# Decoder trunk on one Trainium2 core: weight halves split four half slabs ahead in five buffers, the RG-LRU product on VectorE, its gate weights on ScalarE's queue

## The chip, the cores and the metric

The kernel runs on one core of one Trainium2 chip. The core has a matrix engine (TensorE; PE in the profile, PEld for its weight loads), a vector engine (VectorE; DVE), an engine for activation functions (ScalarE; ACT), a general one (GpSimd; POOL) and one that only issues transfers (SyncE; SP). Each works through its own queue of instructions in order, and they wait for each other by semaphores. On chip there are two memories, SBUF for operands and PSUM for what TensorE adds up; 16 DMA engines move data between SBUF and the chip's main memory, HBM. The metric is device time in microseconds (us) for one run of the whole program.

## The reference

Two layers of a decoder trunk on 256 tokens of width 1024, all in float32. Every layer has three sub-layers, each modulated by vectors that come from a conditioning vector `c`, and each followed by a residual sum and a layer norm:

```python
mod = silu(c) @ mod_w[l] + mod_b[l]                  # nine vectors of 1024
x = LN(ALPHA * x + 0.5 * (1 + g1) * swiglu(x * (1 + sc1) + sh1))
x = LN(ALPHA * x +       (1 + g2) * mixer (x * (1 + sc2) + sh2))
x = LN(ALPHA * x + 0.5 * (1 + g3) * swiglu(x * (1 + sc3) + sh3))
```

`swiglu` is `(silu(gate) * up) @ w_out` with 2816 hidden columns. The mixer of layer 0 ("even") runs an RG-LRU and a gated linear attention (GLA) side by side; that of layer 1 ("odd") is latent attention. The RG-LRU is what one part of the change touches:

```python
r, i = sigmoid(x @ w_a + b_a), sigmoid(x @ w_x + b_x)     # blocks of 64 x 64
log_a = -8 * r * softplus(-lam)
u = sqrt(-expm1(2 * log_a)) * (i * x)
h[t] = exp(log_a[t]) * h[t-1] + u[t]                      # over the 256 tokens
```

## The kernel before

Activations lie transposed: 128 features on the partitions, 256 tokens along a row, eight such tiles (`k` or `f`) for the width of 1024.

**Weights.** All weight matrices are cut into tiles of 128x128 and stored in the order in which TensorE uses them (`PLAN`, lines 108 to 162). Sixteen tiles are a slab of 1 MB, eight a half slab. Float32 precision comes from splitting each operand into a high and a low half of a reduced type (float32r): a product is three matmuls, high x high, high x low and low x high (`mm3`, lines 403 to 409; each 128x128 by 256 columns). So each half slab of weights, once it has landed, is split: ScalarE copies it into `whi` (line 338), VectorE subtracts that copy and writes the rest into `wlo` (line 339). One half slab serves 24 matmuls.

**Class Stream** (lines 300 to 398) runs this pipeline. Raw slabs land in `wraw`, five buffers, which they share with the modulation weights (`modw`, 1 MB each, two columns' worth). `next` hands out weights; when a new half slab `s` is reached it calls `conv_to(s + 1 + AHEAD)`, with `AHEAD = 3`, which emits the splits up to three half slabs further on, after `dma_to` has emitted the transfers of the slabs for them and of up to `RAW = 4` beyond. `whi` and `wlo` have four buffers each, so a split can start when TensorE has finished the half slab four before it. Right behind the splits, `reduce` (line 388) multiplies a modulation weight slab by `silu(c)` and sums it on VectorE; these sums are due by a table (`MOD_TARGETS`) and their results go to the modulation vectors.

**Order of work.** The program only lists instructions. A planner then puts them in order for each engine: it goes through them by priority, which is the place in the listing, simulates when each could start, and gives each engine the ready instruction of highest priority. `tc.high_priority()` moves an instruction forward in that order, `manual_schedule` fixes the order of some engines, and `queue_behind` puts one instruction behind another. On the chip each engine then keeps that order, whatever is ready.

**Buffers in SBUF.** `flat0` and `flat1` (line 452) are two areas of 8 x `FROW` floats a row, `FROW = 320`, used in turn for partial sums, for the scaled `y` of a boundary (`self.ya`, line 546, eight rows of 256 tokens and two extra columns), and in the mixers. The conditioning vector first lands in a buffer of the tag `junk` (line 275), whose other use is the discarded output of `reduce`.

**Boundary** (lines 514 to 678) is what happens between sub-layers. While the last projection's eight tiles `f` come out of TensorE, `tile_out` computes `y = psum * gate + ax` on VectorE (line 581), squares it on ScalarE (585), and adds up sums and squares (588, 589). To keep the statistics exact, the values of tile 0 are used as a shift: `shift_out` (line 559) copies `y` of tile 0 on ScalarE (`yr`, 564), TensorE averages it over the features (566), ScalarE copies the result (`shift`, 569), GpSimd subtracts it from the seven other residual tiles `ax` (571), and VectorE from tile 0 itself (572). Each `y` of tiles 1 to 7 needs its `ax` after that subtraction.

**Even mixer** (lines 790 to 1055). Its steps run in the order of `EVEN_STEPS`; `R` and `S` are the two halves of the RG-LRU, four tiles each. `rglru` loads a tile's gate weights (`rgt`, line 829, 128 KB, from SyncE's queue, two buffers), convolves, multiplies by them (835, 836), applies the gates on ScalarE, and then for all four tiles at once, 128x1024, computes the decay and the input on VectorE (844 to 850). The last product, by the convolved `x`, is on GpSimd (851); the scans over the tokens follow on VectorE (853).

## Time and profile before

| | before |
|---|---|
| median of three runs | 1037.29 us (1035.79 to 1043.17) |
| the profiled execution: its own time | 1033.83 us |
| its span, first to last instruction | 1032.1 us |
| PE busy | 995.5 us, 96% |
| PEld busy | 972.8 us, 94% |
| DVE busy | 884.7 us, 86% |
| ACT busy | 612.5 us, 59% |
| POOL busy | 54.8 us, 5% |
| read from HBM | 256.18 MB |

A row of a timeline reads: start in us from the span's start, busy us, engine, source line, operation, what it writes and reads, how many in a row, and in brackets the idle time before it and what ended that. A row of waits reads: engine and line, what it waited for, total us, how often, the longest. A row of a stretch reads: its limits and length, busy us and number of instructions for PE, PEld, DVE, ACT and POOL, the granted clock as a share, the busy share of the DMA engines, and GB/s. A row for one line of the source gives the shortest, median and longest duration in ns and the first and last start.

### The profile page before, as it was taken

How to read it: one execution, taken by the hardware profiler on the slowest of the kernel's cores; microseconds unless marked ns; L12 is line 12 of the kernel's file. 1: busy time of each engine (PE TensorE's matmuls, PEld its weight loads, DVE VectorE, ACT ScalarE, POOL GpSimd, SP SyncE). 2: the span in 40 equal slices, each digit the busy share in tenths (PEclk: the TensorE clock that was granted, in tenths of full speed). 3: DMA queues.
4: the chain of work that ended last, by engine and by line, in shares of the span. 5: the costliest groups of instructions: out<-in, count | busy, mean ns of one | idle time of the engine just before them, and what ended most of it. 6: DMA issues, size and time to landing. Idle time of an engine off the chain costs nothing.

```text
span 1032.1 us, 20703 instructions
## 1 busy us (share of the span) xinstructions
PE 995.5 (96%) x8338; PEld 972.8 (94%) x8338; DVE 884.7 (86%) x1491; ACT 612.5 (59%) x1023; POOL 54.8 (5%) x72
## 2 busy tenths in 40 slices
PE   6999999999999989999999999999999999999995
PEld 5999999998899979999999999999998889999995
DVE  5789999797998989999998899998888799666664
ACT  4746654567886656745545665455559666545543
POOL 0000010000001020000030000002000200000200
PEclk9999999999999999999999999999999999999998
DMA  9998798554466943699977469898743146665621
GB/s 342 366 339 319 257 368 309 208 204 169 170 264 242 350 185 142 245 361 373 365 279 286 166 251 371 322 359 321 286 167 129 73 164 245 246 224 187 243 83 41
DMA packets 38578, 258.57 MB, mean 251 GB/s; under 512 B 4289, under 2 KB 6849, under 8 KB 7762
## 3 DMA queue, kind: packets, MB, share of 16 engines
q1 hardware_dynamic: 38482, 257.25, 66.7%
q8 instruction: 65, 1.06, 0.4%
q14 instruction: 31, 0.25, 0.1%
HBM read 256.18 MB, written 1.05 MB: 249 GB/s over the span
## 4 chain that ended last, share of the span: by engine, by line
PE 82%; DVE 11%; issue 2%; ACT 2%; DMA 2%; POOL 0%; SPq 0%; DVEq 0%; ACTq 0%
PE mm L409 25%; PE mm L407 25%; PE mm L408 25%; DVE wlo L339 4%; DVE junk L388 2%; DMA wraw<-modw 1%; ACT whi L338 1%; DVE flat L557 1%; DVE yy L581 1%; PE ax L408 1%; PE ax L407 1%; PE ax L409 1%; DVE acc L589 1%; DVE flat L731 0%; DMA rgt<-rgw 0%
## 5 line engine op out<-in xcount | busy, mean ns | idle before, releaser
L339 DVE TENSOR_TENSOR wlo<-wraw,whi 128x1024 fp32r<-128x1024 f32 x340 | 416.7, 1233 | 81.3 <-ACT whi L338 80.8
L338 ACT ACTIVATE whi<-wraw 128x1024 fp32r<-128x1024 f32 x340 | 357.6, 1058 | 212.4 <-PE mm L408 138.0
L407 PE MATMUL mm<-uhi,whi 128*128 128x256 f32 x1672 | 461.4, 278 | 11.5 <-ACT uhi L444 6.0
L409 PE MATMUL mm<-uhi,wlo 128*128 128x256 f32 x1672 | 460.1, 277 | 3.6 <-DVE wlo L339 3.6
L408 PE MATMUL mm<-ulo,whi 128*128 128x256 f32 x1672 | 462.1, 277 | 0.7 <-DVE ulo L445 0.6
L407 PEld LDWEIGHTS mm<-uhi,whi 128*128 128x128 f32 x1672 | 313.6, 188 | 14.9 <-ACT uhi L444 7.9
L409 PEld LDWEIGHTS mm<-uhi,wlo 128*128 128x128 f32 x1672 | 313.8, 188 | 4.2 <-DVE wlo L339 4.1
L408 PEld LDWEIGHTS mm<-ulo,whi 128*128 128x128 f32 x1672 | 314.8, 188 | 1.5 <-DVE ulo L445 1.2
L409 PE MATMUL mm<-hhi,wlo 128*128 128x256 f32 x704 | 194.6, 276 | 1.9 <-DVE wlo L339 1.9
L408 PE MATMUL mm<-hlo,whi 128*128 128x256 f32 x704 | 194.4, 276 | 0.0
L407 PE MATMUL mm<-hhi,whi 128*128 128x256 f32 x704 | 194.3, 276 | 0.0
L388 DVE CUSTOM_DVE_ANT_0 junk<-wraw,cact,cols 128x1024 bf16<-128x1024 f32 x144 | 184.9, 1284 | 5.7 <-DMA wraw<-modw 5.0
L409 PEld LDWEIGHTS mm<-hhi,wlo 128*128 128x128 f32 x704 | 132.1, 188 | 2.3 <-DVE wlo L339 2.3
L407 PEld LDWEIGHTS mm<-hhi,whi 128*128 128x128 f32 x704 | 132.2, 188 | 0.0
L408 PEld LDWEIGHTS mm<-hlo,whi 128*128 128x128 f32 x704 | 132.2, 188 | 0.0
L571 POOL TENSOR_TENSOR ax<-ax,shift 128x256 f32<-128x256 f32 x42 | 42.2, 1039 | 734.7 <-ACT shift L569 734.7
L444 ACT ACTIVATE hhi<-h 128x256 fp32r<-128x256 f32 x88 | 35.9, 413 | 44.3 <-DVE h L702 43.2
L585 ACT ACTIVATE ysq<-yy 128x256 f32<-128x256 f32 x42 | 17.4, 414 | 51.8 <-DVE yy L581 50.0
L702 DVE SCALAR_TENSOR_TENSOR h<-mm,sg 128x256 f32<-128x256 f32 x75 | 30.9, 418 | 7.9 <-PE mm L409 7.9
L581 DVE SCALAR_TENSOR_TENSOR yy<-mm,gate,ax 128x256 f32<-128x256 f32 x48 | 22.8, 478 | 16.2 <-PE mm L409 15.0
L445 DVE TENSOR_TENSOR hlo<-h,hhi 128x256 fp32r<-128x256 f32 x88 | 36.0, 417 | 0.0
L429 ACT ACTIVATE sg<-mm 128x256 f32<-128x256 f32 x75 | 27.4, 366 | 3.0 <-DVE h L702 1.7
(288 smaller groups left out, 1088.1 us busy)
## 6 DMA issues: line engine op xcount, KB each, us to landing
wraw<-wst SPq DMA_DIRECT2D x169, 1024.0 KB, 5.8
wraw<-modw SPq DMA_DIRECT2D x71, 1024.0 KB, 6.5
wraw<-modw SPq DMA_DIRECT2D x2, 512.0 KB, 5.4
yy<-xT SPq DMA_DIRECT2D x8, 128.0 KB, 6.8
wraw<-wst SPq DMA_DIRECT2D x2, 512.0 KB, 7.9
rgt<-rgw SPq DMA_DIRECT2D x8, 128.0 KB, 3.7
outT<-yy SPq DMA_DIRECT2D x3, 256.0 KB, 2.6
outT<-yy SPq DMA_DIRECT2D x2, 128.0 KB, 2.6
```

The lines of the kernel that those rows point to most:

```text
L338: act.activation(hi, raw, AF.Copy)
L339: i = vec.tensor_tensor(lo, raw, hi.bitcast(F32), SUB)
L388: i = vec.tensor_tensor_reduce(junk, t, cact, 1.0, col("mod_b", (l * NMOD + v) * KD + j), MULT, ADD, self.modcols[(l, v)][:, j:j + 1])
L407: pe.matmul(ps, hi, mh, start=start, stop=False, skip_group_check=shared)
L408: pe.matmul(ps, hi, ml, start=False, stop=False, skip_group_check=shared)
L409: pe.matmul(ps, lo, mh, start=False, stop=stop, skip_group_check=shared)
L429: i = act.activation(out, in_, func, **kw)
L444: act.activation(hi, src, AF.Copy)
L445: vec.tensor_tensor(lo, src, hi.bitcast(F32), SUB)
L571: pool.tensor_tensor(ax[:, j, :], ax[:, j, :], shift, SUB)
L581: vec.scalar_tensor_tensor(y, ps, self.gate[:, f:f + 1], ax[:, f, :], MULT, ADD)
L702: vec.scalar_tensor_tensor(h, pu, bu, sg, ADD, MULT)
```

## The change

- `AHEAD` goes from 3 to 4, and `whi` and `wlo` from four buffers to five: splits are listed one half slab earlier and have a buffer more. The raw buffers stay at five.
- `FROW` goes from 320 to 272. The rows of `self.ya` then start 258 floats apart instead of 320.
- The conditioning vector's first buffer moves from `junk` to `flat0`.
- The copy `yr` in `shift_out` gets high priority.
- In `rglru`, `rgt` has three buffers instead of two, its transfers are issued by ScalarE instead of SyncE, and the product of line 851 runs on VectorE instead of GpSimd.

```diff
-FROW = 320
+FROW = 272
...
-    whi = ctx.enter_context(tc.tile_pool(name="whi", bufs=4))
+    whi = ctx.enter_context(tc.tile_pool(name="whi", bufs=5))
...
-    wlo = ctx.enter_context(tc.tile_pool(name="wlo", bufs=4))
+    wlo = ctx.enter_context(tc.tile_pool(name="wlo", bufs=5))
...
-    crow = T(wk, [1, DM], tag="junk", bufs=1)
+    crow = T(main, [1, DM], tag="flat0")
...
-        AHEAD = 3
+        AHEAD = 4
...
-                self.ya = [flat(q, F32R).rearrange("p (k c) -> p k c", k=KD) for q in range(2)]
+                self.ya = [flat(q, F32R)[:, :KD * (SEQ + 2)].rearrange("p (k c) -> p k c", k=KD) for q in range(2)]
...
-            act.activation(yr, y, AF.Copy)
+            with tc.high_priority():
+                act.activation(yr, y, AF.Copy)
...
-                    mm3(ps[:, :SEQ + 2], W.next((m, k, f)), [t[:, k, :SEQ + 2] for t in self.ya], k == 0, k == KD - 1)
+                    mm3(ps[:, :SEQ + 2], W.next((m, k, f)), [t[:, k, :] for t in self.ya], k == 0, k == KD - 1)
...
-                    rgt = T(ew, [P, 2, P], tag="rgt")
-                    sync.dma_start(rgt, rgw[j])
+                    rgt = T(ew, [P, 2, P], tag="rgt", bufs=3)
+                    act.dma_start(rgt, rgw[j])
...
-                pool.tensor_tensor(tz, tz, xc, MULT)
+                vec.tensor_tensor(tz, tz, xc, MULT)
```

## The prediction

> **What bounds the kernel now.** I read the page's busy shares first, then who TensorE waited for, then those waits one by one in the timeline, and last the queues that ended them.

> ```profile
> PE 995.5 (96%) x8338; PEld 972.8 (94%) x8338; DVE 884.7 (86%) x1491; ACT 612.5 (59%) x1023; POOL 54.8 (5%) x72
> PE mm L409 <- DVE wlo L339: 6.5, 6, 1.5
> PE mm L407 <- ACT uhi L444: 6.0, 1, 6.0
> PE mm L407 <- DVE yy L581: 3.1, 2, 1.9
> PE mm L407 <- ACT whi L338: 2.2, 2, 1.4
> ```

> The first row gives 1032.1 - 995.5 = 36.6 us in which TensorE does nothing, and the change takes no matmul away, so this is all there is to win. The other rows (total us, times, longest) say what it waited for: 6.5 us for low halves of weights (`wlo`, VectorE), 3.1 for the boundary's `yy`; the 6.0 and the 2.2 lie in the start, before the first two and at two later weight slabs. The single waits in the timeline, with the idle time in brackets:

> ```profile
> 125.20 0.38 PE L409 MATMUL mm<-uhi,wlo 128*128 128x256 f32 x1 [1.04 <-DVE wlo L339]
> 164.93 0.38 PE L409 MATMUL mm<-hhi,wlo 128*128 128x256 f32 x1 [1.21 <-DVE wlo L339]
> 171.35 0.39 PE L409 MATMUL mm<-hhi,wlo 128*128 128x256 f32 x1 [0.68 <-DVE wlo L339]
> 273.93 0.38 PE L409 MATMUL mm<-uhi,wlo 128*128 128x256 f32 x1 [1.02 <-DVE wlo L339]
> 278.45 0.38 PE L409 MATMUL mm<-uhi,wlo 128*128 128x256 f32 x1 [1.50 <-DVE wlo L339]
> 349.79 0.39 PE L409 MATMUL mm<-ya,wlo 128*128 128x256 f32 x1 [1.06 <-DVE wlo L339]
> 378.10 0.38 PE L407 MATMUL mm<-uhi,whi 128*128 128x256 f32 x1 [1.20 <-DVE yy L581]
> 386.07 0.38 PE L407 MATMUL mm<-uhi,whi 128*128 128x256 f32 x1 [1.92 <-DVE yy L581]
> 835.65 0.46 PE L597 MATMUL ax<-acc,ones_dm 128*128 128x256 f32 x1 [1.33 <-DVE acc L588]
> 837.03 0.70 PE L598 MATMUL ax<-acc,ones_dm 128*128 128x256 f32 x2 [0.71 <-DVE acc L589]
> ```

> Six waits for `wlo` (1.04 + 1.21 + 0.68 + 1.02 + 1.50 + 1.06 = 6.51 us), two for `yy` (3.12), two in the statistics behind the odd mixer (2.04). Busy time by stretch (us, PE, PEld, DVE, ACT, POOL, then clock and DMA) shows which stage each lies in:

> ```profile
> 60.00:70.00 10.00, 10.00 (x90) 10.00 (x90) 6.69 (x12) 5.29 (x8) 0.00 (x0) 1.00 0.97 357
> 160.00:170.00 10.00, 8.79 (x77) 8.60 (x77) 10.00 (x28) 5.90 (x10) 0.00 (x0) 1.00 0.73 265
> 240.00:250.00 10.00, 10.00 (x45) 8.17 (x44) 8.54 (x14) 7.60 (x11) 0.00 (x0) 1.00 0.40 130
> 270.00:280.00 10.00, 7.48 (x63) 7.09 (x62) 10.00 (x14) 6.64 (x12) 2.40 (x1) 1.00 0.30 105
> 340.00:350.00 10.00, 8.94 (x79) 8.74 (x78) 10.00 (x18) 7.57 (x13) 0.00 (x0) 1.00 0.95 351
> 1020.00:1030.00 10.00, 0.84 (x4) 0.30 (x2) 7.06 (x18) 4.94 (x11) 2.09 (x3) 0.68 0.31 104
> ```

> Where TensorE waits for weights, VectorE is busy 10.00 of 10 us; ahead of those stretches it has room (6.69 of 10 at 60, 8.54 at 240). The last row is the tail, 9.16 us of idle TensorE in which no weight is converted: the change leaves it.

> **Five buffers, four ahead.** What holds a conversion back where VectorE has room:

> ```profile
> ACT whi L338 <- PE mm L408: 138.0, 124, 2.6
> 47.45 1.06 ACT L338 ACTIVATE whi<-wraw 128x1024 fp32r<-128x1024 f32 x1 [0.72 <-PE mm L408]
> 50.17 1.06 ACT L338 ACTIVATE whi<-wraw 128x1024 fp32r<-128x1024 f32 x1 [1.66 <-PE ax L408]
> 48.55 1.23 DVE L339 TENSOR_TENSOR wlo<-wraw,whi 128x1024 fp32r<-128x1024 f32 x1 [1.16 <-ACT whi L338]
> ```

> In 124 cases ScalarE sat until a matmul gave a buffer back, so the fifth buffer will be used. Two conversions in that state lie 50.17 - 47.45 = 2.72 us apart, TensorE's time for a half slab. With four buffers a half slab starts when the one four before it is done and is due three later, 3 x 2.72 = 8.16 us; it is ready at 48.55 + 1.23 = 49.78, 2.33 us after its start, so the lead is 5.83 us. Five buffers make it 8.55.

> What that closes depends on VectorE. The work is the same; one conversion (1.23 us) is done while there is room and is then missing from the busy stretch, and in VectorE's queue each `wlo` stands one half slab earlier, ahead of work whose results TensorE wants later. Counted wait by wait:
> - 125.20: the lead was full at 60 us, where VectorE has 3.3 us of room in ten. 1.04 is less than the 1.23 taken out of the queue: closed, 1.04.
> - 164.93 and 171.35, 1.89 together: the stretch at 160 shows VectorE full, and the first wait has used up the lead, so I count the one conversion alone, 1.23, and leave 0.66. Bounds: 0 (VectorE is the limit and the wait only moves) and 1.89.

> The raw buffers stay five. A half slab converted earlier gives its raw buffer back earlier, which can only bring the next transfer forward; at the start TensorE waits for transfers and modulation sums, the same in both, so I count 0 there.

> **The product from GpSimd to VectorE.** It occurs twice, once for each half of the RG-LRU:

> ```profile
> 269.09 1.22 DVE L850 SCALAR_TENSOR_TENSOR ya<-ya,ya 128x1024 f32<-128x1024 f32 x1
> 270.39 2.40 POOL L851 TENSOR_TENSOR ya<-ya 128x1024 f32<-128x1024 f32 x1 [61.11 <-DVE ya L850]
> 270.56 3.31 DVE L339 TENSOR_TENSOR wlo<-wraw,whi 128x1024 fp32r<-128x1024 f32 x1
> 311.47 3.33 POOL L851 TENSOR_TENSOR ya<-ya 128x1024 f32<-128x1024 f32 x1 [38.68 <-DVE ya L850]
> 314.83 2.44 DVE L853 TENSOR_TENSOR_SCAN flat<-ya,ya 128x256 f32<-128x256 f32 x4 [2.30 <-POOL ya L851]
> ```

> VectorE's queue gets one 128x1024 product; the same shape takes 1.22 on line 850. In the first half the `wlo` beside the product took 3.31 instead of 1.23, so taking the product off GpSimd gives 2.08 back and costs 1.22: VectorE is 0.86 us earlier. This very `wlo` is the one of the wait at 273.93. With the conversion done ahead in the room at 240 (1.46 us) that is 0.86 + 1.23 = 2.09 against waits of 1.02 + 1.50 = 2.52; and the scans, which stood before the next `wlo`, are no longer held either. I take 2.52, with 0.86 as the low bound. [...]

> In the second half VectorE waited 2.30 for GpSimd before the scans and will compute 1.22: 1.08 us earlier, into the stretch that stays busy until 349.79. With the earlier conversion, 1.08 + 1.23 = 2.31, more than the wait of 1.06: closed. Bounds 0 and 1.06.

> **Gate weights on ScalarE's queue, three buffers.**

> ```profile
> SPq L829 <- PE ax L836: 4.3, 3, 3.0
> 257.70 0.38 SPq L325 DMA_DIRECT2D wraw<-wst  x1
> rgt<-rgw SPq DMA_DIRECT2D x8, 128.0 KB, 3.7
> 252.56 1.06 ACT L338 ACTIVATE whi<-wraw 128x1024 fp32r<-128x1024 f32 x1 [0.51 <-PE mm L986]
> ```

> SyncE was held 4.3 us in three waits for a buffer that the gate matmuls read, and a weight transfer stood behind the longest, at 257.70. That hold moves to ScalarE, in front of conversions and the gates' activations, though with three buffers the third load needs no wait. No row shows an issue on ScalarE; SyncE's is 0.38, so eight cost about 3.0, and with all the old waits 7.3 us of ScalarE's time. I count 0: ScalarE waited for TensorE itself at 252.56, it is busy 7.60 of 10 us at 240, and the lead covers one hold of 3.0. Without that cover the cost is 7.3; on the other side SyncE, freed by up to 3.0 us, gains nothing, because no wait above is for `wraw`.

> **The copy `yr` at high priority.**

> ```profile
> 372.55 0.48 DVE L581 SCALAR_TENSOR_TENSOR yy<-mm,gate,ax 128x256 f32<-128x256 f32 x1 [0.59 <-PE mm L409]
> 372.49 1.06 ACT L338 ACTIVATE whi<-wraw 128x1024 fp32r<-128x1024 f32 x1 [0.99 <-PE mm L408]
> 373.45 0.40 ACT L564 ACTIVATE shift<-yy 128x256 fp32r<-128x256 f32 x1
> 375.22 0.39 ACT L569 ACTIVATE shift<-ax 128x256 f32<-128x256 f32 x1 [0.41 <-PE ax L566]
> 375.68 6.67 POOL L571 TENSOR_TENSOR ax<-ax,shift 128x256 f32<-128x256 f32 x7 [60.88 <-ACT shift L569]
> L571 POOL TENSOR_TENSOR ax<-ax,shift x42: 717/919/1783, 151.2 to 977.6; 128x256 f32<-128x256 f32 x42
> ```

> `yy` of tile 0 is there at 373.03; the copy starts at 373.45 because a conversion was put ahead of it. So 0.42 goes from the way to the shift, the subtractions on GpSimd and the `yy` that TensorE waited 1.20 for. Bounds 0 and 3.12 (the wait of 1.92 stands behind the same seven subtractions; no row says how much of it is theirs). In the boundaries behind an FFN TensorE did not wait for `yy`: 0.

> Rows of `flat` packed closer (258 instead of 320 columns), the conditioning row in `flat0` instead of `junk`: same instructions, same shapes; 0.

> **Sum.** 1.04 + 1.23 + 2.52 + 1.06 + 0.42 = 6.27 us. The profiled execution has a span of 1032.1 and a time of 1033.83, 3.46 below the median 1037.29 of the runs (1035.79 to 1043.17). On its own time 1027.6; on the median 1031.0.

> **Rivals.**
> - VectorE stays the limit: the waits move along the busy stretches, and only its own saving counts, 0.86 + 1.06 = 1.92. Or the planner leaves the conversions where they were, and the edit does not do what it says. For: three of the six stretches above have VectorE at 10.00. Against: 124 conversions started on a freed buffer. Time 1035.4, between 1033.5 and 1037.5.
> - The boundaries close too: all six weight waits, both `yy` waits and the two behind the odd mixer, 6.51 + 3.12 + 2.04 = 11.67. For: one conversion less stands among that work. Against: a conversion per 2.72 us stays in VectorE's queue there. Time 1025.6, up to 1028.
> - Slower: collisions in the mixers' boundaries. The order of VectorE's queue is new, and one conversion stands nearer to the seven subtractions. Their duration ranges from 0.717 to 1.783 and was 6.67 / 7 = 0.95 in the even boundary. If every one meets a VectorE instruction that went first, each takes 1.783: 7 x 0.83 = 5.8 us per boundary, straight onto the `yy` that TensorE waits for, and 11.6 in the two behind the mixers. With the rest of the gain, 5.85, this gives 1043.0; without it 1048.9. It decides if VectorE has a two-input instruction running at each subtraction's start; against it, the median of all 42 is 0.919, so most meet none. [...]

> **How the numbers follow.** Forecast 0.55 (1028.5 to 1033.5), VectorE the limit 0.20, boundaries too 0.14, slower 0.11. The range 1026 to 1038 holds the first two, half of the third and little of the fourth, 0.82. One per cent, about what a measurement of this kernel can tell from no change, is 10.4 us: faster means under 1026.9. Two thirds of the third case lie there, 0.09, and the low edge of the forecast with the runs' spread adds 0.08: 0.17. Slower means over 1047.7, half of the fourth case: 0.06. Within: 0.77.

> **What would show it.** Right: the waits of `mm L409` for `wlo` fall from 6.5 to about 0.7; the lines of 125, 274, 278 and 350 are gone; no line 851 on GpSimd, no `wlo` of 3.31, the scans wait for nothing; TensorE idle near 30 us with its busy time unchanged. The copy step is right if the wait of 1.20 shrinks by about 0.4. Wrong: `wlo` waits of the same total at later places (first rival); conversions whose durations differ from 1.06 and 1.23, which would speak of the new addresses; ScalarE held by a gate load for longer than the lead of 8.55; subtractions near 1.78 (third rival).

## The result: 0.5% slower, and the profile after

The changed kernel takes 1042.63 us (median of 20 runs, 1035.89 to 1047.03); the kernel before, run beside it, 1036.74 (20 runs, 1034.21 to 1043.17). The ratio is 1.005, with a 95% interval of 1.0036 to 1.0064. The forecast was 1031.0, in a range that ended at 1038: the sign was wrong. The profiled execution of the changed kernel has a time of its own of 1047.03 us, the longest of the 20, and a span of 1045.3; that of before had 1033.83 and 1032.1. So the two profiles lie 13.2 us apart, where the medians lie 5.9 apart. Behind line 563 the numbers of the changed kernel are one higher than before's.

The page first: busy times, and the granted clock in 40 slices.

```profile
PE 1002.0 (96%) x8338; PEld 979.3 (94%) x8338; DVE 885.7 (85%) x1493; ACT 610.7 (58%) x1023; POOL 52.9 (5%) x70
PEclk9999999999989999999999999999999999999998
```

TensorE does the same 8338 matmuls and is busy 6.5 us longer (995.5 before), and its idle time is 1045.3 - 1002.0 = 43.3 us, 6.7 more than the 36.6 of before. Half of the loss is idle time, and half is matmuls that ran longer. The 8 among the nines of the clock row, at about 300 us, says where. Then who TensorE waited for (total us, times, longest), leaving out the start and the tail:

```profile
PE ax L836 <- DMA rgt<-rgw: 5.3, 1, 5.3
PE mm L407 <- DVE yy L582: 3.1, 2, 1.9
PE ax L567 <- ACT shift L565: 3.1, 1, 3.1
PE mm L407 <- ACT yy L429: 1.8, 1, 1.8
PE mm L409 <- DVE wlo L339: 1.7, 2, 1.4
PE ax L942 <- DVE la L975: 1.2, 1, 1.2
```

The waits for `wlo` have gone from 6.5 us to 1.7, much as forecast. But the first row is new: one gate matmul waited 5.3 us for its weights to land. So are the third, fourth and sixth (`la` is an operand of the GLA that VectorE computes). The timeline shows that wait and what leads up to it:

```profile
292.71 0.59 PE L837 MATMUL ax<-ya,rgt 128*128 128x256 f32 x2
293.34 0.47 ACT L429 ACTIVATE sg<-ax,hba 128x256 f32<-128x256 f32 x1 [0.36 <-PE ax L837]
293.34 0.33 SPq L325 DMA_DIRECT2D wraw<-wst  x1
294.48 0.33 SPq L372 DMA_DIRECT2D wraw<-modw  x1
297.32 0.33 ACTq L830 DMA_DIRECT2D rgt<-rgw  x1
306.01 1.19 PE L836 MATMUL ax<-ya,rgt 128*128 128x256 f32 x2 [5.29 <-DMA rgt<-rgw]
308.09 0.47 ACT L429 ACTIVATE sg<-ax,hba 128x256 f32<-128x256 f32 x1 [7.62 <-PE ax L837]
321.37 0.39 PE L407 MATMUL mm<-uhi,whi 128*128 128x256 f32 x1 [1.84 <-ACT yy L429]
```

With three buffers the eighth gate load needs the buffer of the fifth, which the matmul at 292.71 gives back at 293.30. ScalarE issues the load at 297.32, 4.0 us later: from 293.34 on its queue holds ten activations of the gates (the first is shown), and the issue stands behind them. By then two 1 MB weight transfers of SyncE are on their way (issued at 293.34 and 294.48; the first is about to land, at 298.1), and a third is issued 0.26 us behind the gate load, at 297.58. The 128 KB take 8.5 us, until 305.9, and the third slab 8.6, until 306.2. ScalarE in turn waits 7.62 us for the late matmul's result, and the activation that is to empty a PSUM tile stands behind it: TensorE waits another 1.84 at 321.37. Before, with two buffers, SyncE issued the last two loads ahead of the weight slab. The eighth landed 3.5 us after its issue, at 298.1, and the matmuls found both there:

```profile
293.80 1.19 SPq L829 DMA_DIRECT2D rgt<-rgw  x2
295.18 0.33 SPq L325 DMA_DIRECT2D wraw<-wst  x1
298.38 0.59 PE L835 MATMUL ax<-ya,rgt 128*128 128x256 f32 x2
```

How long the eight gate loads took from issue to landing, first of the changed kernel, then of before:

```profile
DMA to landing us min/median/max: 2.0/4.6/8.5
```

```profile
DMA to landing us min/median/max: 1.9/3.7/6.1
```

The 8.5 is the eighth's. The medians decide nothing: with SyncE's queue and three buffers (below) the median is 4.6 too, and TensorE waits for none.

The other half of the loss is in the stretches of the changed kernel behind that wait and behind the wait for `shift` (limits, length, busy us of PE, PEld, DVE, ACT, POOL, then the granted clock and the DMA engines):

```profile
303.50:313.90 10.40, 7.89 (x33) 7.57 (x34) 2.93 (x6) 4.15 (x6) 0.00 (x0) 0.51 0.51 208
719.00:724.00 5.00, 4.56 (x25) 4.56 (x26) 3.56 (x4) 3.10 (x6) 3.31 (x4) 0.66 0.97 390
```

In this trace the clock stands at one of two values: 1.00 from 300 to 303.5, 0.50 from 303.6 to 313.8, 1.00 from 313.9 on; 0.50 again from 720.1 to 723.4 and from 849.8 to 853.1, and in the tail. So a mean of 0.51 over 10.40 us is half clock for 2 x 0.49 x 10.40 = 10.2 us; 0.66 over 5.00 is 3.4 us of it; from 849 to 854 the mean is 0.66 once more. Together, ahead of the tail, that is 17 us at half speed. The matmuls of lines 407 to 409 start 0.21 us apart from 720.0 to 723.2 and 0.11 to 0.12 apart behind that. The lengths of half clock in the runs below are estimates, from the mean of a stretch in the same way, with 1.00 and 0.50 as the two values. Of the first 10.2, 2.4 us lie within the wait itself (a mean clock of 0.80 over the 6 us from 300), where nothing is lost; the other 14.6 cost up to 7.3 us, and 6.5 us more busy time is what the page shows. Before had full clock from the start to the tail (1.00 up to 1023.5 us, 0.50 behind it).

The wait for `shift` near 716 is another matter. There the `yy` of tile 0 stood in VectorE's queue behind two modulation sums, the first of which (its row is shown) waited 1.31 us for its transfer, and a split:

```profile
714.78 1.28 DVE L388 CUSTOM_DVE_ANT_0 junk<-wraw,cact,cols 128x1024 bf16<-128x1024 f32 x1 [1.31 <-DMA wraw<-modw]
718.46 0.48 DVE L582 SCALAR_TENSOR_TENSOR yy<-mm,gate,ax 128x256 f32<-128x256 f32 x1
```

### The profile page after: what moved, and what is told of

The parts are those of the page before. It is cut to its first block, busy times and chain, and to the rows that moved or that the text cites. A ratio compares the mean times of both kernels' runs of the same rounds, so it can differ in the third digit from the quotient of the medians.

```text
span 1045.3 us, 20613 instructions
## 1 busy us (share of the span) xinstructions
PE 1002.0 (96%) x8338; PEld 979.3 (94%) x8338; DVE 885.7 (85%) x1493; ACT 610.7 (58%) x1023; POOL 52.9 (5%) x70
## 3 DMA queue, kind: packets, MB, share of 16 engines
q8 instruction: 65, 1.06, 0.4%
q10 hardware_dynamic: 1152, 1.05, 0.4%
HBM read 256.18 MB, written 1.05 MB: 246 GB/s over the span
## 4 chain that ended last, share of the span: by engine, by line
PE 76%; DVE 13%; DMA 4%; ACT 3%; issue 3%; POOL 0%; SPq 0%; DVEq 0%; ACTq 0%
PE mm L408 23%; PE mm L407 23%; PE mm L409 23%; DVE wlo L339 4%; DVE junk L388 3%; DMA wraw<-modw 3%; DMA rgt<-rgw 1%; ACT whi L338 1%; PE ax L942 1%; DVE h L703 1%; DVE yy L582 0%; DVE acc L590 0%; DVE flat L732 0%; PE ax L409 0%; PE ax L407 0%
## 5 line engine op out<-in xcount | busy, mean ns | idle before, releaser
L339 DVE TENSOR_TENSOR wlo<-wraw,whi 128x1024 fp32r<-128x1024 f32 x340 | 413.9, 1226 | 78.2 <-ACT whi L338 76.3
L407 PE MATMUL mm<-uhi,whi 128*128 128x256 f32 x1672 | 462.1, 279 | 13.3 <-ACT uhi L444 6.1
L408 PE MATMUL mm<-ulo,whi 128*128 128x256 f32 x1672 | 462.6, 278 | 0.5 <-DVE ulo L445 0.5
L338 ACT ACTIVATE whi<-wraw 128x1024 fp32r<-128x1024 f32 x340 | 355.7, 1056 | 180.7 <-PE mm L408 136.3
L409 PE MATMUL mm<-uhi,wlo 128*128 128x256 f32 x1672 | 460.4, 277 | 0.3 <-DVE wlo L339 0.3
L407 PEld LDWEIGHTS mm<-uhi,whi 128*128 128x128 f32 x1672 | 314.1, 189 | 16.5 <-ACT uhi L444 7.9
L408 PEld LDWEIGHTS mm<-ulo,whi 128*128 128x128 f32 x1672 | 315.4, 189 | 1.3 <-DVE ulo L445 1.0
L409 PEld LDWEIGHTS mm<-uhi,wlo 128*128 128x128 f32 x1672 | 314.4, 189 | 0.6 <-DVE wlo L339 0.5
L409 PE MATMUL mm<-hhi,wlo 128*128 128x256 f32 x704 | 195.2, 277 | 1.4 <-DVE wlo L339 1.4
L407 PE MATMUL mm<-hhi,whi 128*128 128x256 f32 x704 | 195.1, 277 | 0.0
L408 PE MATMUL mm<-hlo,whi 128*128 128x256 f32 x704 | 195.0, 277 | 0.0
L409 PEld LDWEIGHTS mm<-hhi,wlo 128*128 128x128 f32 x704 | 132.9, 189 | 1.6 <-DVE wlo L339 1.6
L408 PEld LDWEIGHTS mm<-hlo,whi 128*128 128x128 f32 x704 | 133.0, 189 | 0.0
L407 PEld LDWEIGHTS mm<-hhi,whi 128*128 128x128 f32 x704 | 132.9, 189 | 0.0
L572 POOL TENSOR_TENSOR ax<-ax,shift 128x256 f32<-128x256 f32 x42 | 46.0, 1129 | 852.9 <-ACT shift L570 852.9
L444 ACT ACTIVATE hhi<-h 128x256 fp32r<-128x256 f32 x88 | 35.8, 413 | 64.8 <-DVE h L703 64.7
## 6 DMA issues: line engine op xcount, KB each, us to landing
rgt<-rgw ACTq DMA_DIRECT2D x8, 128.0 KB, 4.6
yy<-xT SPq DMA_DIRECT2D x8, 128.0 KB, 8.0
outT<-yy SPq DMA_DIRECT2D x2, 128.0 KB, 2.6
```

The lines of the kernel that those rows point to most:

```text
L338: act.activation(hi, raw, AF.Copy)
L339: i = vec.tensor_tensor(lo, raw, hi.bitcast(F32), SUB)
L407: pe.matmul(ps, hi, mh, start=start, stop=False, skip_group_check=shared)
L408: pe.matmul(ps, hi, ml, start=False, stop=False, skip_group_check=shared)
L409: pe.matmul(ps, lo, mh, start=False, stop=stop, skip_group_check=shared)
L444: act.activation(hi, src, AF.Copy)
```

## The experiments

Every time is a median, with its ratio to the kernel before, run on the same chip (1035.42, 1035.52 or 1036.48 us there), and the 95% interval of that ratio. Versions from different chips are compared by their ratios; 0.1% is 1.04 us.

**The gate loads back on SyncE's queue, all else changed.**

```diff
-                    act.dma_start(rgt, rgw[j])
+                    sync.dma_start(rgt, rgw[j])
```

> The changed kernel with the gate weights' transfers back on SyncE's queue, three buffers kept. Theory 1 (the late load): in the changed kernel the eighth gate load left ScalarE's queue at 297.3 us, landed 8.5 us later, TensorE waited 5.3 us for it and then ran 10.2 us at half clock. On SyncE's queue it goes ahead of the weight transfers that are issued after it, so the wait of 5.3 and the half clock around 304 us go; time 1042.6 less 5.3 and about 4, so 1033 to 1035, ratio to before 0.996 to 0.999. Theory 2 (the copy at high priority, with its wait of 3.1 us at 716 us): nothing changes but the last load, 1041 to 1043, ratio about 1.005.

1030.32 us, 0.996 (0.9944 to 0.9976). One word moves the time from 0.5% above before to 0.4% below it: 9 us by the ratios (12.3 by the medians). Its waits, and rows of its timeline:

```profile
PE mm L407 <- DVE yy L582: 3.1, 2, 1.9
PE mm L409 <- DVE wlo L339: 1.7, 2, 1.4
```

```profile
163.81 0.39 PE L409 MATMUL mm<-hhi,wlo 128*128 128x256 f32 x1 [1.40 <-DVE wlo L339]
277.94 0.43 PE L942 MATMUL ax<-la,bc 128*128 128x64 f32 x2 [1.05 <-DVE la L975]
291.09 0.59 PE L837 MATMUL ax<-ya,rgt 128*128 128x256 f32 x2
291.71 0.33 SPq L830 DMA_DIRECT2D rgt<-rgw  x1
292.25 0.33 SPq L325 DMA_DIRECT2D wraw<-wst  x1
294.41 0.61 PE L836 MATMUL ax<-ya,rgt 128*128 128x256 f32 x2
```

No wait for `rgt`, and a mean clock of 0.996, as in before, whose half clock lies in the tail alone; from 290 to 320 it is 1.00. The matmul that frees the eighth load's buffer ends at 291.68; SyncE issues the load 0.03 us later, ahead of the next slab, and at 294.41, 2.7 us on, TensorE uses it without a wait. The rest of the change thus gains much of what was forecast, and the move of the queue takes back twice that.

**The queue's move alone, on the kernel before** (three buffers and ScalarE's queue, nothing else).

```diff
-                    rgt = T(ew, [P, 2, P], tag="rgt")
-                    sync.dma_start(rgt, rgw[j])
+                    rgt = T(ew, [P, 2, P], tag="rgt", bufs=3)
+                    act.dma_start(rgt, rgw[j])
```

> The kernel before with one part of the change alone: gate weights on ScalarE's queue, three buffers. Theory 1 (the late load): the eighth load is late here too, TensorE waits 3 to 6 us for it and the clock halves behind it; 1040 to 1046, ratio 1.004 to 1.009. Theory 2 (the copy): no change, 1036 to 1038, ratio 1.000.

1041.2 us, 1.0046 (1.0027 to 1.0064): some 5 us slower than before by itself. From its waits, and a stretch of its clock:

```profile
PE ax L941 <- DVE la L974: 2.3, 2, 1.2
PE ax L835 <- DMA rgt<-rgw: 2.1, 2, 1.3
```

```profile
283.00:287.00 4.00, 3.90 (x20) 3.90 (x21) 4.00 (x8) 2.84 (x6) 0.00 (x0) 0.57 0.69 262
```

Here the lead is shorter and the gate loads are late twice, by 1.25 and 0.81 us, less than the 3 to 6 expected; the clock is halved once, 2 x 0.43 x 4 = 3.4 us, behind the two waits for `la` and not behind a gate load. In the changed kernel the same edit costs more, 9 us by the ratios, with one long wait where this has two short ones.

**More buffers on ScalarE's queue**, four and then eight, so that the issue waits for no matmul.

```diff
-                    rgt = T(ew, [P, 2, P], tag="rgt", bufs=3)
+                    rgt = T(ew, [P, 2, P], tag="rgt", bufs=4)
```

> The changed kernel with four buffers for the gate weights, still on ScalarE's queue: the eighth load waits for matmuls of the first half and is issued some 20 us earlier; four loads instead of three stand ahead of the first slabs. Theory 1 (late because of buffer and place in ScalarE's queue): no wait for a gate load, 1031 to 1034, ratio 0.996 to 0.999, between the versions with eight buffers there and with SyncE's queue. Rival (any load on a second queue is slowed by the slabs): the wait stays at 2 to 5 us, 1038 to 1043.

> The changed kernel with eight buffers for the gate weights, transfers still on ScalarE's queue: no load waits for a buffer, all eight are issued in the first microseconds. Theory 1 (the late load): no wait for a gate load, no half clock near 304 us; but five more loads of 128 KB compete with the first slabs, 0.66 MB at some 400 GB/s, 1.6 us later at the start; time 1034 to 1037, ratio 0.997 to 1.000. Theory 2 (the copy): 1041 to 1044, ratio about 1.005.

Four: 1032.24 us, 0.9967 (0.9951 to 0.9983). Eight: 1034.51, 0.9989 (0.9977 to 1.0002). In neither does TensorE wait for a gate load; with four the last are issued between 269.8 and 277.4, long before their use. So ScalarE's queue does no harm in itself once the issue isn't tied to a late buffer. What is left shows at the start, where the loads that need no buffer run at once. First the changed kernel, then the one with four buffers, then the one on SyncE's queue, with the first matmul of each:

```profile
1.41 0.86 ACTq L830 DMA_DIRECT2D rgt<-rgw  x2
3.03 3.37 SPq L325 DMA_DIRECT2D wraw<-wst  x2
12.10 1.22 PE L407 MATMUL mm<-uhi,whi 128*128 128x256 f32 x4 [5.93 <-ACT uhi L444]
```

```profile
13.33 1.22 PE L407 MATMUL mm<-uhi,whi 128*128 128x256 f32 x4 [7.26 <-ACT uhi L444]
```

```profile
3.02 1.21 SPq L325 DMA_DIRECT2D wraw<-wst  x2
11.73 1.23 PE L407 MATMUL mm<-uhi,whi 128*128 128x256 f32 x4 [5.41 <-ACT uhi L444]
```

Gate loads at 1.4 us, which are needed at 250, hold up the first weight slabs: two issues of SyncE take 3.37 us instead of 1.21, and TensorE's first matmul comes 0.4 us later with three buffers, 1.6 with four, and 3.2 with eight (14.97). The 1.6 with four buffers is about what this version stands behind that on SyncE's queue (0.7 by the ratios, 1.9 by the medians), and the 3.2 with eight about what that one does (3.0 by the ratios). The 0.4 with three is about what the start differs by between executions without such loads: 12.03 before, 11.74 in the version with the product alone.

**The issue moved forward in ScalarE's order.**

```diff
-                    act.dma_start(rgt, rgw[j])
+                    with tc.high_priority():
+                        act.dma_start(rgt, rgw[j])
```

> The changed kernel with the gate weights' loads at high priority on ScalarE's queue, three buffers: the eighth load stands in front of the twelve gate activations (some 4 us) behind which it was issued at 297.3, so it should be issued near 293.5, when its buffer comes free. Theory L (late because of its place in ScalarE's queue): it lands some 4.6 us later (the median of the eight), before TensorE comes at 300.7; no wait, 1032 to 1035, the 1.5 us of the loads at the start remaining; ratio 0.997 to 0.999. Theory S (slow because it shares the DMA engines with three slabs of another queue): 8.5 us to land, 302, a wait of 1.3 us and some half clock; 1035 to 1038, ratio 1.000 to 1.002.

1040.54 us, 1.0023 (1.0001 to 1.0045): more than either theory had forecast.

```profile
294.91 0.36 ACTq L831 DMA_DIRECT2D rgt<-rgw  x1
294.92 0.33 SPq L325 DMA_DIRECT2D wraw<-wst  x1
300.37 0.67 PE L837 MATMUL ax<-ya,rgt 128*128 128x256 f32 x2 [2.19 <-DMA rgt<-rgw]
```

The issue now follows the buffer at once (it came free at 294.87), the wait shrinks from 5.29 to 2.19, and the time by 2.8 us by the ratios, about what the intervals leave unsure. But the load still takes 5.3 us, from 294.91 to 300.2: a 1 MB slab was issued 0.01 us behind it on the other queue and another 2.7 us ahead of it, at 292.19. Late issue and slow landing each have a share. The median stays 9.6 us above that of two buffers on SyncE's queue, on the same chip (the next runs); this profile, one of the shorter runs of its kernel, has further waits of 2.00 (`la`) and 2.9 (`ut`, in the GLA's output), and a mean clock of 0.993 where the version on SyncE's queue has 0.996: some 6 us more at half clock, an estimate from the two means and spans (1034.2 and 1027.1). None follows the 2.19 for the gate load: matmuls of lines 407 to 409 start 0.12 us apart there. What brings these two waits is open, and so is why this version's median stays so high.

**Is the third buffer needed, and are eight better, on SyncE's queue?** Two buffers as before, and eight.

```diff
-                    rgt = T(ew, [P, 2, P], tag="rgt", bufs=3)
-                    act.dma_start(rgt, rgw[j])
+                    rgt = T(ew, [P, 2, P], tag="rgt")
+                    sync.dma_start(rgt, rgw[j])
```

> The changed kernel with the gate loads exactly as before the change (SyncE's queue, two buffers), all else kept. If only the queue did harm: as with three buffers on SyncE's queue, 1030 to 1032, ratio 0.995 to 0.997. Rival (the third buffer gave a part of that gain): 1032 to 1035, ratio 0.997 to 1.000.

> The changed kernel with the gate loads on SyncE's queue and eight buffers: all eight issued in a row during the first feed-forward block, none waits for a buffer. If the place in the queue is all that matters: 1029 to 1031, ratio 0.994 to 0.996, no wait for a gate load. Rival (1 MB in one go delays the slabs behind it where TensorE needs them): a new wait for weights near 110 us, 1031 to 1034.

Two: 1030.96 us, 0.9941 (0.9922 to 0.9959). Eight: 1031.75, 0.995 (0.9931 to 0.9968). Both agree with three buffers within the intervals. A hold of SyncE for a gate buffer, which was the one thing to be gained by the move, costs nothing that shows here; the profile with two has one wait of 0.60 for a gate load, at 258, and those with three and eight none. These three are the fastest versions; the measurements don't rank them.

**Is the halved clock a cost of its own?** Matmuls into the same PSUM tile, whose results the gate matmul then overwrites, put into the idle time ahead of the last gate matmul as fillers: 44, and when these didn't fill it, 90.

```diff
+                    if j == KD - 1:
+                        for _ in range(90):
+                            pe.matmul(gp[:, :SEQ], uhi[:, 0, :P], uhi[:, 0, :], start=True, stop=True)
                     pe.matmul(gp[:, :SEQ], rgt[:, 0, :], x, start=True, stop=True)
```

> The changed kernel with 44 matmuls more (128x128 by 256, uhi by itself, into the PSUM tile that the next matmul overwrites) right in front of the gate matmul that waits for the eighth load; the result is unchanged. They take 44 x 0.114 = 5.0 us, about the wait of 5.3, so TensorE arrives when the load does, and the load itself is as late as before. Theory A (the idle time halves TensorE's clock, and that is nearly half of the loss): no half clock near 304 us, time 1042.6 less some 4, 1037 to 1040. Theory B (the clock has nothing to do with the wait): half clock in the same place as often, time 1042 to 1045.

> As with 44 matmuls in front of the late gate matmul, but 90: 10.2 us of busy TensorE, more than the wait of 5.3, so TensorE does not idle there. Against the changed kernel it adds 10.2 and saves 5.3. Theory A (idle time halves the clock): no half clock between 295 and 320 us, which saves some 4 more, so 1043 to 1044.5, ratio to before about 1.008. Theory B (the clock has nothing to do with it): 1047 to 1048.5, ratio about 1.012.

With 44: 1044.13 us, 1.0069 (1.0043 to 1.0096). A wait of 2.92 was left and the clock was still halved (a mean of 0.57 from 306 to 314): this run decided nothing. With 90: 1042.3 us, 1.0052 (1.0032 to 1.0072), the ratio of the changed kernel. Theory B's 1.012 lies outside; theory A's 1.008 was some 3 us too high by the ratios.

```profile
296.11 10.96 PE L838 MATMUL ax<-uhi 128*128 128x256 f32 x90
306.91 0.60 PE L839 MATMUL ax<-ya,rgt 128*128 128x256 f32 x2
```

```profile
306.00:314.00 8.00, 8.00 (x55) 7.50 (x54) 4.72 (x8) 4.47 (x10) 0.00 (x0) 1.00 0.41 159
```

Eleven microseconds of useless matmuls cost no time that shows: the two ratios, this one and the changed kernel's, differ by 0.2 us, with intervals of 1.4 and 2.1 us to each side. They fill the 5.3 of the wait; had the wait been all, the other 5.7 would have made the kernel slower. Two things pay for them. The clock is 1.00 from 306 to 314, where the changed kernel lost half of its 7.8 us at half speed, 3.9. And the wait of 1.84 at 321.37 is gone. Together, with that wait put down to the late load, 5.3 + 3.9 + 1.8 = 11.0 us is its cost in that profile.

**The lead alone, on the kernel before** (`AHEAD`, five buffers, the packed rows and the moved vector).

```diff
-        AHEAD = 3
+        AHEAD = 4
```

> The kernel before with one part of the change alone: four ahead, five buffers, with the smaller flat rows and the moved conditioning row that make room. The prediction's terms for it: 1.04 + 1.23 + 1.06, and of the pair at 274 and 278 about 1.2, so 4.5 us; ratio 0.995 to 0.997. Rival (VectorE is the limit, the waits move): within 1 us of before, ratio 0.999 to 1.001.

1034.75 us, 0.9988 (0.9972 to 1.0003): a gain of about 1 us, within error. The 4.5 expected lie outside the interval, and the rival's time came true. Its waits for `wlo` fall (the one at 350 is gone), but two for `la` come in, and the clock behind them is halved:

```profile
279.27 0.43 PE L941 MATMUL ax<-la,bc 128*128 128x64 f32 x2 [1.34 <-DVE la L974]
281.13 0.69 PE L941 MATMUL ax<-la,bc 128*128 128x64 f32 x2 [1.20 <-DVE la L974]
```

```profile
281.00:288.00 7.00, 6.87 (x33) 6.87 (x34) 4.59 (x9) 2.03 (x4) 0.00 (x0) 0.52 0.73 277
```

That is 2 x 0.48 x 7 = 6.7 us at half speed, about 3.4 us lost. The rival's mechanism came true in part: the two waits for `la`, 2.54 together, stand where before had 2.52 for `wlo`.

**The product on VectorE alone, on the kernel before.**

```diff
-                pool.tensor_tensor(tz, tz, xc, MULT)
+                vec.tensor_tensor(tz, tz, xc, MULT)
```

> The kernel before with one part of the change alone: the RG-LRU product on VectorE. The prediction's terms for it: 0.86 off the wait at 274 and 1.06, the wait at 350, so 1.9 us; no stretched subtraction of 3.3 us; ratio 0.997 to 0.999. Rival (VectorE is full there, so one more product is one more wait): 0 to 2 us slower, ratio 1.000 to 1.002.

1032.72 us, 0.9969 (0.9956 to 0.9983): a gain of about 3 us (1.8 to 4.6 by the interval). The `wlo` behind the product takes 1.22 instead of 3.31, and the scans wait for nothing. Of the two waits at 274 and 278 one is left, and the one at 350 is gone:

```profile
277.42 0.38 PE L409 MATMUL mm<-uhi,wlo 128*128 128x256 f32 x1 [1.08 <-DVE wlo L339]
```

**Without the high priority of `yr`.**

```diff
-            with tc.high_priority():
-                act.activation(yr, y, AF.Copy)
+            act.activation(yr, y, AF.Copy)
```

> The changed kernel without the high priority of the copy yr. Theory 1 (the late load): the wait for the gate load stays near 5 us with half clock behind it; the wait at 716 us may go (3.1 us and 1.7 of half clock), so 1038 to 1043, ratio 1.001 to 1.006. Theory 2 (the copy): the wait at 716 goes and is the whole difference to before, 1037 to 1038, ratio about 1.000.

1042.62 us, 1.0062 (1.0039 to 1.0085): no different from the changed kernel's 1.005. Its waits for `yy` are 1.20 and 1.97. Its profile, of the shortest of its six runs, has a wait of 3.04 for the gate load, with 6.8 us of half clock behind it (a mean of 0.53 over 7.2 us), and none for `shift`.

## Why the prediction was wrong, point by point

**The step that failed** is "I count 0" for the gate weights on ScalarE's queue. It weighed what the move costs ScalarE (eight issues and the holds, at most 7.3 us) and what it frees on SyncE. It did not ask when the load would land for TensorE. Two parts of that could be had from the profile of before. The issue joins the queue of an engine that computes, behind the ten activations of the tiles before it. And it leaves the queue in which it stood ahead of the next weight slab. The row of the page with 3.7 us from issue to landing is a median of eight loads (1.9 to 6.1) and said nothing of the one that matters: the eighth landed in 3.5 us before, in at most 2.7 on SyncE's queue with three buffers, and in 8.5 in the changed kernel. What that term is worth is the distance between the changed kernel and the one on SyncE's queue, 9 us by the ratios and 12 by the medians. "The lead covers one hold of 3.0" was right for the weights and beside the point.

**Had the prediction seen the wait, it would have had half of the price**: the 5.3 us of idle time brought 3.9 us by the halved clock and 1.8 by a second wait, and 11 us of other work in its place cost nothing.

**The sum of the rest held, its parts less so.** Taking the version with three buffers on SyncE's queue against before, by TensorE's waits: at 125 from 1.04 to 0.28 (forecast: to 0); at 164 and 171 from 1.89 to 1.40 (to 0.66); at 274 and 278 from 2.52 to 1.05 (to 0), where the `wlo` waits are gone as forecast but a wait for `la` came in, a result of VectorE that stands behind splits in the same busy stretch; at 350 1.06 gone, as forecast. The start, counted 0, gained 1.4: a wait of 0.85 before the third slab is gone and the first is shorter, 5.96 to 5.41. The sum is 0.76 + 0.49 + 1.47 + 1.06 + 1.4 = 5.2 against 6.27, and the spans are 1032.1 and 1027.1. The start's part isn't firm: in the versions with two and eight buffers on SyncE's queue a wait of 0.8 before the third slab is still there, and the start gains 0.5. The medians of these three versions, 1030.3 to 1031.8, lie about the 1031.0; by the ratios they gain 4.1 to 6.1 us. That agreement is partly luck: the start made up for what the busy stretches kept, and of the two main parts the lead alone brought 1 us where 4.5 was counted, the product 3 where 1.9 was.

**The product** gained about 3 us alone, with no scan held by GpSimd; its own share in the forecast, 0.86 + 1.06 = 1.92, lies at the low end of the interval.

**The copy `yr`**, 0.42, was worth nothing: the wait of 1.20 is 1.16 to 1.20 with and without it. The step took it that the high priority would put the copy ahead of the conversion. It did not: in the changed kernel and in the version on SyncE's queue ScalarE's order at this boundary is that of before. In the latter `yy` is there at 367.99, and the copy starts 0.41 us later, behind the same conversion (0.42 before):

```profile
367.44 1.06 ACT L338 ACTIVATE whi<-wraw 128x1024 fp32r<-128x1024 f32 x1 [0.98 <-PE mm L408]
368.40 0.40 ACT L565 ACTIVATE shift<-yy 128x256 fp32r<-128x256 f32 x1
```

So the bound of 0 came true without the mechanism being tested: what an earlier copy would be worth, no run shows.

**The rivals.** VectorE as the limit is partly true: 1.4 us stayed at 164, and the waits at 274 moved to `la`. The boundaries did not close; the waits for `yy` are 3.1 to 3.2 us in all versions. The collisions in the mixers' boundaries, my only slower case, did not come: those same 3.1 us, and a median of 0.923 for the subtractions of the changed kernel (0.919 before). The trace of before bears out what it rested on: all ten of the 42 subtractions that took over 1.5 us (1.50 to 1.78) started while a conversion or a modulation sum, 128x1024, was running on VectorE. But of the seven in each of the two mixers' boundaries one was such (1.73 and 1.72 us), and one was in the changed kernel (1.72 and 1.71). The kernel became slower by a mechanism that no rival named, although the list of what would prove me wrong had ScalarE "held by a gate load for longer than the lead"; what mattered was the load held by ScalarE.

**Left open.** The wait for `shift` of 3.1 us is 2.2 with 90 fillers and 0 to 0.7 elsewhere. Two versions that keep the queue's move, with 44 fillers and without the priority of `yr`, have none, so the move alone doesn't bring it. In the changed kernel a modulation slab that landed late stood ahead of it; no run shows what made it late.

## What to carry to other kernels

Before a load moves to another queue, look up two things in the trace: what the new issuing engine computes between the moment the buffer comes free and the issue, and which transfers the load stood ahead of in the old queue. A small load that is needed soon belongs in front of the big ones, in one queue with them (3.5 us to land in before, at most 2.7 with three buffers there, against 8.5 beside them from another queue), or early enough that neither matters (no wait for it with four or eight buffers); and it should not run at the start only because its buffer is free (TensorE's first matmul came 1.6 us later with four buffers, 3.2 with eight). The new wait of TensorE of 5.3 us cost 11.0 here, about twice its length.

## What the runs showed of the hardware

```profile
382.00:387.00 5.00, 5.00 (x32) 5.00 (x31) 3.85 (x7) 1.64 (x3) 0.00 (x0) 0.66 0.32 80
```

```profile
384.00:390.00 6.00, 6.00 (x49) 5.67 (x48) 5.99 (x12) 3.79 (x7) 0.00 (x0) 1.00 0.93 345
```

The lengths are about one, two and three times 3.4 us. A wait of 1.96 us, or two of 1.1 to 1.3 close together, were followed by half clock in some executions, and one of 1.92 and one of 2.19 in others were not; in before none was, of ten from 0.68 to 1.92 long between 125 and 837 us. What decides it, no run here shows. That the idle time is the cause is shown for the long wait, by the fillers; for the short ones it rests on the half clock standing right behind them.

**In the runs of the changed kernel time and missing clock went together.** Of the 20 runs of the changed kernel the shortest, 1035.89 us, had a mean clock of 0.995, and the three above 1045 had 0.986 to 0.988. The part of the clock that is missing, times the span, is 5.2 us in the first and 12.5 to 14.6 in the others. Over all 20 runs the two go together with a correlation of 0.90; the waits ahead of each halving are in that too. One halving of 3.4 us at 0.50 costs up to 1.7, an estimate.

**Beside another queue's slabs the small load landed late.** The eighth gate load, 128 KB, landed in 3.5 us behind another gate load and ahead of a slab in SyncE's queue, and in 8.5 us from ScalarE's queue beside three transfers of 1 MB; from 300 to 306 the DMA engines were 94% busy. At high priority on ScalarE's queue, issued 0.01 us ahead of a slab, it took 5.3. Packets and MB by queue, in the changed kernel from 297 to 306 (q1 is SyncE's, q10 ScalarE's, which carries the one gate load):

```profile
q1 hardware_dynamic: 422, 3.06, 89.2%
q10 hardware_dynamic: 144, 0.13, 5.7%
```

While the 0.13 MB were out, 3.06 MB of slabs went by; the packets of both queues took 94.9% of the time of the 16 engines. A packet of the gate load carries about an eighth of what a slab's does (0.9 and 7.3 KB); whether that sets its share, no run here shows. The move saved nothing here: with two buffers, and so with SyncE held, the kernel was as fast as with three or eight, within the intervals.
